# Two inverses made by VectorE between the last convolutions; triangle products of both directions together; VectorE ahead of ScalarE on the PSUM tiles of G and E

## The chip, the cores and the metric

The kernel runs on one core of a Trainium2 chip. A core has five engines with a queue each, which go on in order and wait for one another by semaphores: TensorE (PE in the profile; PEld are its weight loads), VectorE (DVE), ScalarE (ACT), GpSimd (POOL) and SyncE (SP, which here only starts DMAs). SBUF is the memory on the core, PSUM the one that TensorE writes its products into. The metric is the device time of one execution in microseconds. Before the change it is 1668.08 us, the median of three runs (1666.92 to 1673.68).

## The reference

One step of a two-branch mixer layer. 128 context tokens and 2048 latent tokens (a grid 64 wide), 1024 channels. Half of the channels go through a delta-rule recurrence in both directions (8 heads of 64), the other half through a gated short convolution; both are gated, joined and projected out.

```python
h = _rmsnorm(x, lp['norm_g']) * (1.0 + scale) + shift
proj = h @ lp['w_in']
r, k, v, g_a, b_gate, c_gate, u_conv, g_b = jnp.split(proj, IN_SPLITS, axis=-1)
...
def step(S, inp):
    r_t, w_t, k_t, v_t, kk_t, a_t = inp
    s_kk = jnp.einsum('bdhij,bdhj->bdhi', S, kk_t)
    S = (S * w_t[..., None, :] - s_kk[..., :, None] * (kk_t * a_t)[..., None, :]
         + v_t[..., :, None] * k_t[..., None, :])
    return S, jnp.einsum('bdhij,bdhj->bdhi', S, r_t)
s_final, ys = lax.scan(step, s0.astype(f32), xs)
...
yb = b_gate * _short_conv(c_gate * u_conv, lp['conv_w'], is_latent) * jax.nn.silu(g_b)
u = jnp.concatenate([ya, yb], axis=-1) @ lp['w_out']
return x + gate * u, s_final
```

The result is the normalised layer output for context and latent tokens, and the final context states S.

## The kernel before

The recurrence is computed in chunks of 64 tokens: 34 chunks for each pair of heads and each direction. Within a chunk the delta rule needs the inverse of a unit lower-triangular 64x64 matrix, made from two 32x32 inverses and a few products.

**Phase 1** projects. The tokens are cut into six blocks j (five of 384 tokens and one of 256), handled in three thirds of two blocks; in each third the four groups g of 128 channels are run through `mixA` (r, k, v and everything that the recurrence reads), `gateA`, `convB` and `gateB`. Names of PSUM tiles say what is projected: mmr, mmk, mmv, mmc, mmu, mmgb, mmb and so on; these five-slot tiles are taken in turn, so a product of one block can't start before the tile five earlier has been read. `mixA` calls `triangle` (L368) once for each direction: the products al x be of each chunk and head half, into a PSUM tile psA, each in two 64x64 quadrants of the array (`place`, L37), then three ScalarE copies into a staging tile and two DMAs to the scratch tensors scr_at (the two triangular 32x32 blocks) and scr_lo (the 32x32 block below them). In the last two thirds the list `late` is not empty; spare weight buffers then hold the staging tiles. In the last third, the convolutions and their gates of groups 1 to 3 are left for the end; beside them `early` (L1204) runs, a generator that is advanced by one step after each convolution or gate of a block.

**Phase 2** runs the recurrence in 17 stages, each with 8 chunks of both directions (gi = 0 and 1). A stage first needs its 32x32 inverses: `partI` (L886) loads the triangles of the stage (L919) and `solve` (L921) inverts them on GpSimd by elimination, two rows at a time: a product (L936) and two subtracts (L939) for each of 15 steps. The inverse goes to scr_zt (L940) and comes back as zc (L1003). Stages 0 and 1 are solved in `ahead1` during the last third, stages 2 to 4 in `early`, the rest in `main`. From the inverse and the staged operands, `partU` and `partW` make the tiles zb, F and G, `partB` X and E, and `partS` goes over the eight chunks with the state sv:

- psF -> F, one VectorE instruction (L1017); psG -> fg, four times a stage and half: for each of two tiles and two heads a ScalarE copy of one column half and a VectorE product with a mask of the other (the two lines after L1022);
- psX -> fg, four ScalarE copies with a sign; psE -> E, a ScalarE copy and a VectorE product with a mask for each tile (L1085, L1086);
- psS -> sv, the state's update on VectorE (L1123).

fg has for each direction and operand three slots, of which slot 0 holds constants, and 1 and 2 are filled in turn by even and odd stages. In `main` the order of TensorE is fixed by a string of letters (ROUND), and five PSUM slots go round for F, G, X, E, U and W; in `early`, two. Two engines that read one PSUM tile are kept in the order of the code: the second waits for the first. All the rest of the order on each engine is found by a scheduler that plans with estimated durations, so that a change in the code also moves instructions at other places.

**Phase 3** is the output projection.

Of the kernel before, what the change touches and what calls it, by code (L numbers as in the profile page):

```python
# [54 lines left out]
def phase1(K):  # L55
# [312 lines left out]
    def triangle(g, j, d, al, be, t_):  # L368

        t0, n = BLK[j]  # L370
        nch, c0 = n // 64, t0 // 64
        x, y = (be, al) if d == 0 else (al, be)
        ps = pax.tile([128, 6, 64], F32, tag="ax", name=f"psA{g}_{j}_{d}")
        for u in range(nch):
            for h in range(2):
                r = slice(h * 64, h * 64 + 64)
                T.matmul(ps[place(d, h), u, :], x[r, u * 64:u * 64 + 64], y[r, u * 64:u * 64 + 64], start=True, stop=True)  # L377
        o = t_[:, :].rearrange("p (k u i) -> p k u i", k=2, i=32)
        P.copy(o[:, :, :nch], ps[:, :nch].rearrange("p u (k i) -> p k u i", k=2))
        for r in (slice(32, 64), slice(96, 128)):  # L380
            K.mark = P.copy(o[r, 0, :nch], ps[r, :nch, 32:64]).ins
        nc.sync.dma_start(S["at"][d, g, c0:c0 + nch].rearrange("u s b j i -> (s b j) u i"), o[:, 0, :nch])
        nc.sync.dma_start(S["lo"][d, g * 128:g * 128 + 128, c0:c0 + nch], o[:, 1, :nch])

    def mixA(g, j, ws, hh, lw, pre):
# [23 lines left out]
        kds = []  # L409
        for d in range(2):  # L410
# [43 lines left out]
            triangle(g, j, d, al, be, staging(ta))  # L454
# [294 lines left out]
def phase2(K):  # L749
# [136 lines left out]
    def partI(s, after=None):  # L886

        if s < 4:
# [32 lines left out]
    def solve(s, ab, zt, tmp, dg, after):  # L921

        zf = zt[:].rearrange("p a b -> p (a b)")
        behind(G.memset(zt[:], 0.0), after)
        for h in range(2):
            G.memset(zf[h * 64:(h + 1) * 64, h:512:34], 1.0)

        G.tensor_copy(dg[:], ab[:].rearrange("p j i -> p (j i)")[:, 1:1024:66])
        G.tensor_scalar(zf[0:64, 1:512:34], dg[0:64], -1.0, None, ALU.mult)
        tv = tmp[:].rearrange("p (j m) -> p j m", m=16)  # L930
        G.tensor_tensor(tv, ab[:, :, 0:32:2], dg[:].unsqueeze(1).broadcast_to((128, 32, 16)), ALU.mult)
        G.tensor_tensor(ab[:, :, 1:32:2], ab[:, :, 1:32:2], tv, ALU.subtract)
        for m in range(15):
            j, kn, n = 2 * m, m + 1, 30 - 2 * m
            tv = tmp[:, :kn * 2 * n].rearrange("p (q r i) -> p q r i", r=2, i=n)
            G.tensor_tensor(tv, ab[:, j:j + 2, j + 2:32].unsqueeze(1).broadcast_to((128, kn, 2, n)),  # L936
                            zt[:, :kn, j:j + 2].unsqueeze(3).broadcast_to((128, kn, 2, n)), ALU.mult)
# [266 lines left out]
    def early():  # L1204
# [10 lines left out]
        for gen in (W, W, uu, uu, uu):  # L1215
            next(gen, None)
            yield
# [263 lines left out]
```

## Time and profile before

The profiled execution took 1662.38 us, of which the span from first to last instruction is 1660.6 us. The stages of it (PE idle is the window less PE's busy time):

| stretch, us | what runs | PE busy | PE clock granted |
|---|---|---|---|
| 0 to 98 | loads, modulation, norm of the first blocks | 76.4 | |
| 98 to 748 | first and middle third of phase 1 | 642.5 | |
| 748 to 921 | last third; stages 0 and 1 solved on GpSimd | 166.0 | 0.99 |
| 921 to 1000 | last convolutions and gates, with `early` | 79.0 | 1.00 |
| 1000 to 1335 | phase 2 up to its last rounds | 296.5 | 0.96 to 0.98 |
| 1335 to 1475 | last rounds, output weights prepared | 109.9 | 0.86 |
| 1475 to 1661 | output projection | 178.1 | 0.99 |
| span 1660.6, execution 1662.38 | | 1548.4 | 0.978 |

How to read the rows that follow: a row of the timeline has start, duration, engine, line, operation, out<-in, partitions x elements out<-in, the count of instructions, and in brackets the idle time before it and who ended it. Rows of one tile have min/median/max in ns and the first and last start.

### The profile page before, as it was taken

The numbers are of one execution on the slowest core, as the hardware profiler recorded it, in microseconds if no ns is written. First come the engines' busy times: TensorE is split into PE (matmuls) and PEld (weight loads), VectorE is DVE, ScalarE is ACT, GpSimd is POOL, SyncE is SP. The second block draws the span as 40 slices with busy tenths as digits, with TensorE's granted clock in tenths as the row PEclk, the third lists the DMA queues.
The fourth block names the chain that finished last, engine by engine and source line by source line (L and its number), as shares of the span: only waits on it lengthen the run. The fifth ranks groups of instructions, "written<-read, shape, count | busy, mean of one in ns | idle before, by whom it ended". The sixth has DMA issues, their size and how long they took to land.

```text
span 1660.6 us, 42386 instructions
## 1 busy us (share of the span) xinstructions
PE 1548.4 (93%) x17160; PEld 1417.8 (85%) x17160; DVE 1077.8 (65%) x2122; ACT 767.6 (46%) x1623; POOL 615.9 (37%) x1134
## 2 busy tenths in 40 slices
PE   6899999999999999999999998988889988789998
PEld 2899998999999999999988997777777877668886
DVE  5876978784638776657788534676767765574343
ACT  4544565553425454435554024666576655432222
POOL 0011221110102111112775588888888840022221
PEclk9899999999999999999999999999999979889999
DMA  9677767665746465555858859566676643264342
GB/s 378 211 258 244 254 236 265 215 227 194 217 145 207 165 207 189 188 201 179 269 177 245 273 180 272 150 184 191 171 211 157 193 135 103 65 198 149 137 146 95
DMA packets 237859, 327.23 MB, mean 197 GB/s; under 512 B 91288, under 2 KB 191896, under 8 KB 223584
## 3 DMA queue, kind: packets, MB, share of 16 engines
q1 hardware_dynamic: 231552, 318.02, 59.6%
q0 software_dynamic: 1360, 4.46, 0.7%
q8 instruction: 135, 2.21, 0.5%
q10 hardware_dynamic: 4752, 2.04, 0.5%
q14 instruction: 60, 0.49, 0.1%
HBM read 207.92 MB, written 116.54 MB: 195 GB/s over the span
## 4 chain that ended last, share of the span: by engine, by line
PE 69%; DVE 14%; ACT 7%; issue 5%; DMA 3%; POOL 0%; SPq 0%; DVEq 0%; ACTq 0%; POOLq 0%
PE psu L1351 4%; PE psu L1350 4%; PE psu L1352 4%; PE psE L834 3%; PE psS L834 3%; ACT fg L823 3%; PE psA L377 2%; PE mmc L166 2%; PE mmc L167 2%; PE mmu L166 2%; PE mmc L168 2%; PE mmu L168 2%; PE mmu L167 2%; PE psX L834 2%; PE mmv L166 2%
## 5 line engine op out<-in xcount | busy, mean ns | idle before, releaser
L939 POOL TENSOR_TENSOR zt<-zt,ztmp 128x30 f32<-128x30 f32 (+7 forms) x450 | 179.5, 399 | 35.1
L834 PE MATMUL psE<-fg 128*64 128x128 f32 x2176 | 137.4, 280 | 20.9 <-DVE fg L1025 17.2
L834 PEld LDWEIGHTS psE<-fg 128*64 128x64 f32 x2176 | 123.1, 141 | 27.3 <-issue 22.0
L834 PE MATMUL psS<-sv,E 128*64 128x64 f32 x2176 | 107.1, 236 | 25.1 <-DVE sv L1123 21.7
L834 PEld LDWEIGHTS psS<-sv,E 128*64 128x64 f32 x2176 | 83.5, 143 | 48.2 <-DVE sv L1123 38.5
L329 POOL TENSOR_TENSOR shk<-rawl 128x384 f32<-128x384 f32 (+1 forms) x24 | 24.9, 1037 | 233.8 <-ACT rawl L325 214.6
L936 POOL TENSOR_TENSOR ztmp<-ab,zt 128x60 f32<-128x60 f32 (+7 forms) x195 | 99.7, 511 | 15.3
L823 ACT ACTIVATE fg<-psX 64x512 f32<-64x512 f32 x136 | 80.5, 592 | 40.5 <-PE psX L834 38.4
L1417 POOL TENSOR_TENSOR z<-z,x 128x512 f32<-128x512 f32 x32 | 41.7, 1303 | 139.4 <-DVE z L1413 114.6
L1123 DVE TENSOR_TENSOR sv<-psS,pc 64x128 f32<-64x128 f32 x254 | 67.8, 279 | 38.8 <-PE psS L834 36.2
L1025 DVE TENSOR_TENSOR fg<-psG,consts 64x256 f32<-64x256 f32 x136 | 56.8, 418 | 47.9 <-ACT fg L825 45.1
L329 POOL TENSOR_TENSOR shv<-rawl 128x384 f32<-128x384 f32 (+1 forms) x24 | 20.4, 852 | 161.9 <-ACT rawl L325 153.7
L825 ACT COPY E<-psE 128x256 f32<-128x256 f32 x136 | 47.7, 374 | 52.6 <-PE psE L834 43.5
L166 PE MATMUL mmg<-h,w 128*128 128x384 f32 (+1 forms) x192 | 63.6, 331 | 3.7 <-ACT q1v L327 3.7
L1017 DVE TENSOR_TENSOR F<-psF,consts 128x512 f32<-128x512 f32 x68 | 44.0, 680 | 34.6 <-PE psF L834 34.6
L166 PE MATMUL mmc<-h,w 128*128 128x384 f32 (+1 forms) x192 | 64.3, 335 | 2.3 <-ACT t L423 1.8
L1086 DVE TENSOR_TENSOR E<-psE,consts 128x256 f32<-128x256 f32 x136 | 54.5, 416 | 18.2 <-ACT E L825 16.7
L825 ACT COPY fg<-psG 64x256 f32<-64x256 f32 x136 | 49.9, 367 | 33.5 <-PE psG L834 16.9
L166 PE MATMUL mmb<-h,w 128*128 128x384 f32 (+1 forms) x192 | 63.1, 329 | 1.5 <-ACT ta L436 1.5
L443 POOL COPY pcs<-pp 128x6 f32<-128x6 f32 (+1 forms) x48 | 21.5, 450 | 115.3 <-ACT pp L432 115.0
L166 PE MATMUL mmgb<-h,w 128*128 128x384 f32 (+1 forms) x192 | 63.7, 332 | 0.3 <-ACT q1r L327 0.3
L166 PE MATMUL mmv<-h,w 128*128 128x384 f32 (+1 forms) x192 | 63.4, 330 | 0.2 <-ACT q1r L327 0.2
(316 smaller groups left out, 5144.9 us busy)
## 6 DMA issues: line engine op xcount, KB each, us to landing
w<-scr_wsp SPq DMA_DIRECT2D x68, 1024.0 KB, 5.5
scr_wsp<-w SPq DMA_DIRECT2D x34, 1024.0 KB, 4.9
scr_ops<-pair SPq DMA_DIRECT2D x80, 384.0 KB, 3.0
wr<-in_win SPq DMA_DIRECT2D x34, 512.0 KB, 5.9
o<-scr_ops SPq DMA_DIRECT2D x32, 512.0 KB, 7.0
fg<-scr_ops SPq DMA_DIRECT2D x120, 128.0 KB, 5.0
x<-in_x SPq DMA_DIRECT2D x17, 512.0 KB, 3.8
wadas<-in_wada SPq DMA_DIRECT2D x8, 1024.0 KB, 13.5
```

Source lines behind the costliest of these rows:

```text
L166: T.matmul(ps[:, :n], w[:, 0, k], hh[:, 0, k, :n], start=k == 0, stop=False)
L167: T.matmul(ps[:, :n], w[:, 0, k], hh[:, 1, k, :n], start=False, stop=False)
L168: K.dense = T.matmul(ps[:, :n], w[:, 1, k], hh[:, 0, k, :n], start=False, stop=k == 7).ins
L823: P.activation(dst, src, AF.Copy, scale=-1.0)
L825: P.copy(dst, src)
L834: r = T.matmul(*a, start=True, stop=True, **k)
L936: G.tensor_tensor(tv, ab[:, j:j + 2, j + 2:32].unsqueeze(1).broadcast_to((128, kn, 2, n)), zt[:, :kn, j:j + 2].unsqueeze(3).broadcast_to(( ...
L939: O.solved = G.tensor_tensor(zt[:, :kn, j + 2:32], zt[:, :kn, j + 2:32], tv[:, :, r], ALU.subtract).ins
L1123: r = V.tensor_tensor(dst, sp[gi][0:64, q], B.pc[0:64, d, 2 * p:2 * p + 2, c:c + 1].broadcast_to((64, 2, 64)), ALU.mult)
L1350: T.matmul(ps[:], mh[:, n], hi[:, cs], start=start and n == 0, stop=False)
L1351: T.matmul(ps[:], mh[:, n], lo[:, cs], start=False, stop=False)
L1352: T.matmul(ps[:], ml[:, n], hi[:, cs], start=False, stop=stop and n == 3)
```

## The change

Three edits.

- `triangle` becomes `triangles`: it takes a list of directions and makes their products by turns, chunk by chunk and head by head. In the first third it is still called once for each direction; from the middle third on, once for both.
- `solve` becomes a generator for an engine to be named. GpSimd's solves use it as before. `by_vector` runs it on VectorE for stages 3 and 4 in `early`, with slot 2 of fg as scratch memory; the store of the inverse goes to SP's queue. GpSimd solves 2 and then 5 there, and 6 on in `main`.
- In the evacuation of psG and of psE the VectorE product stands ahead of the ScalarE copy.

```diff
-    def triangle(g, j, d, al, be, t_):
+    def triangles(g, j, todo):
...
         for u in range(nch):
+            us = slice(u * 64, u * 64 + 64)
             for h in range(2):
                 r = slice(h * 64, h * 64 + 64)
-                T.matmul(ps[place(d, h), u, :], x[r, u * 64:u * 64 + 64], y[r, u * 64:u * 64 + 64], start=True, stop=True)
+                for p_, (d, al, be, _) in zip(ps, todo):
+                    x, y = (be, al) if d == 0 else (al, be)
+                    T.matmul(p_[place(d, h), u, :], x[r, us], y[r, us], start=True, stop=True)
...
-            triangle(g, j, d, al, be, staging(ta))
+            todo.append((d, al, be, staging(ta)))
+            if not late or d:
+                triangles(g, j, todo)
+                todo = []
...
-    def solve(s, ab, zt, tmp, dg, after):
+    def solve_steps(eng, s, ab, zt, tmp, dg, after):
...
         for m in range(15):
             j, kn, n = 2 * m, m + 1, 30 - 2 * m
             tv = tmp[:, :kn * 2 * n].rearrange("p (q r i) -> p q r i", r=2, i=n)
-            G.tensor_tensor(tv, ab[:, j:j + 2, j + 2:32].unsqueeze(1).broadcast_to((128, kn, 2, n)),
-                            zt[:, :kn, j:j + 2].unsqueeze(3).broadcast_to((128, kn, 2, n)), ALU.mult)
+            eng.tensor_tensor(tv, ab[:, j:j + 2, j + 2:32].unsqueeze(1).broadcast_to((128, kn, 2, n)),
+                              zt[:, :kn, j:j + 2].unsqueeze(3).broadcast_to((128, kn, 2, n)), ALU.mult)
             for r in range(2):
-                O.solved = G.tensor_tensor(zt[:, :kn, j + 2:32], zt[:, :kn, j + 2:32], tv[:, :, r], ALU.subtract).ins
-        G.dma_start(S["zt"][s].rearrange("h u s b q i -> (h u s b) (q i)"), zf)
+                last = eng.tensor_tensor(zt[:, :kn, j + 2:32], zt[:, :kn, j + 2:32], tv[:, :, r], ALU.subtract).ins
+            if m % 4 == 0:
+                yield
+        if eng is G:
+            O.solved = last
+        (G.dma_start if eng is G else D)(S["zt"][s].rearrange("h u s b q i -> (h u s b) (q i)"), zf)
+
+    def by_vector(s, d):
+
+        x = [B.fg[d][:, k, 2].rearrange("p h u t -> p (h u t)") for k in range(2)]
+        ab = x[0].rearrange("p (j i) -> p j i", i=32)
+        load_I(s, ab, K.dense)
+        yield
+        yield from solve_steps(V, s, ab, x[1][:, 0:512].rearrange("p (a b) -> p a b", b=32), x[1][:, 512:1024],
+                               O.rI.tile([128, 16], F32, tag="dgv", name=f"dgv{s}", bufs=1), K.dense)
...
+                    V.tensor_tensor(g.gs[H[1 - h], g.op, h, us], ps[gi][r, :, 64:128], B.mG[r, g.d].unsqueeze(1).broadcast_to((64, 4, 64)), ALU.mult)
                     copy(g.gs[H[1 - h], 0, h, us], ps[gi][r, :, 0:64])
-                    V.tensor_tensor(g.gs[H[1 - h], g.op, h, us], ps[gi][r, :, 64:128], B.mG[r, g.d].unsqueeze(1).broadcast_to((64, 4, 64)), ALU.mult)
...
+                    V.tensor_tensor(to(H[1]), of(H[1]), B.mE[:, g.d].unsqueeze(1).broadcast_to((128, 4, 64)), ALU.mult)
                     copy(to(H[0]), of(H[0]))
-                    V.tensor_tensor(to(H[1]), of(H[1]), B.mE[:, g.d].unsqueeze(1).broadcast_to((128, 4, 64)), ALU.mult)
...
         partI(2)
         B.back = O.solved
+        vec = (x for k in range(2) for x in by_vector(3 + k, k))
+        next(vec)
         yield
         sts[0] = partL(0, K.dense)
-        yield
-        partI(3, K.dense)
+        next(vec)
         yield
         W, uu, bb = partW(0, sts[0]), partU(0, sts[0]), partB(0, sts[0])
         for gen in (W, W, uu, uu, uu):
             next(gen, None)
+            next(vec, None)
+            next(vec, None)
             yield
-        partI(4, B.back)
+        partI(5, B.back)
         for gen in (bb, W, W):
             next(gen, None)
+            next(vec, None)
             yield
+        for _ in vec:
+            pass
```

How this moves instructions, at three places.

VectorE, among the last convolutions, around the masked copies of G of stage 0 (pv, ob, vcarry belong to the convolutions; F and psG to stage 0). Before:

```order
L541 COPY pv_4_10219<-vcarry 128x128
L1017 TENSOR_TENSOR F_10158<-psF_0_0_10140,consts 128x512
L1017 TENSOR_TENSOR F_10160<-psF_1_0_10141,consts 128x512
L535 TENSOR_TENSOR pv_4_10219<-ct_4_10191,mmu_10193 128x384
L88 TENSOR_SCALAR ob_4_10218<-pv_4_10219,dv 128x384
L550 COPY vcarry<-pv_4_10219 128x128
L517 SCALAR_TENSOR_TENSOR ob_4_10218<-pv_4_10219,dv,ob_4_10218 128x384
L519 SCALAR_TENSOR_TENSOR ob_4_10218<-pv_4_10219,dv,ob_4_10218 128x384
L1025 TENSOR_TENSOR fg_9816<-psG_0_0_10226,consts 64x256
```

In the changed kernel (fg_9816 and fg_9817 on both sides of the arrow are the scratch of stage 3's and stage 4's inverse):

```order
L950 TENSOR_TENSOR fg_9816<-fg_9816 128x8x16
L547 COPY pv_4_10247<-vcarry 128x128
L942 TENSOR_TENSOR fg_9817<-fg_9817,dgv_10256 128x512
L947 TENSOR_TENSOR fg_9816<-fg_9816 128x252
L943 TENSOR_TENSOR fg_9817<-fg_9817 128x512
L950 TENSOR_TENSOR fg_9816<-fg_9816 128x9x14 x2
L947 TENSOR_TENSOR fg_9816<-fg_9816 128x240
L1048 TENSOR_TENSOR fg_9816<-psG_0_0_10141,consts 64x256
L1048 TENSOR_TENSOR fg_9817<-psG_1_0_10142,consts 64x256
L950 TENSOR_TENSOR fg_9816<-fg_9816 128x10x12
L1048 TENSOR_TENSOR fg_9816<-psG_0_0_10141,consts 64x256
```

The first inverse is spread between the evacuations, F stands behind its first half, and psG's evacuation stands ahead of the next convolution's mmu where it stood behind it. On TensorE the products of psF and psG moved with this: psF now stands within a gate's products mmb and psG within the next convolution's mmc, where each stood behind a whole projection.

SP, from the second of the last convolutions on (w are weights, scr_zt the inverses, ob the convolutions' results). Before:

```order
L127 DMA w_891_10508<-scr_wsp 128x2048
L919 DMA ab_10572<-scr_at 32x1024 x3
L127 DMA w_892_10510<-scr_wsp 128x2048
L883 DMA a_9813<-scr_lo 128x256 x2
L581 DMA scr_mixT<-ob_4_10218 128x384
L127 DMA w_903_10742<-scr_wsp 128x2048
L127 DMA w_904_10744<-scr_wsp 128x2048
```

In the changed kernel:

```order
L955 DMA scr_zt<-fg_9816 128x512
L925 DMA o_9815<-scr_at 32x1024
L127 DMA w_891_10646<-scr_wsp 128x2048
L882 DMA o_9814<-scr_ops_57 128x2x512
L127 DMA w_892_10648<-scr_wsp 128x2048
...
L955 DMA scr_zt<-fg_9817 128x512
L127 DMA w_899_10823<-scr_wsp 128x2048
L998 DMA fg_9817<-scr_ops_58 64x2x256 x2
L127 DMA w_900_10825<-scr_wsp 128x2048
```

The two stores, which wait for VectorE's last instruction of an inverse, now stand ahead of two pairs of weight loads. The loads of fg from scr_ops, which fill slot 2 for stage 1, stood earlier in the queue; they now come behind the stores, since slot 2 is the scratch.

VectorE, in the middle of phase 2 (one round: E and sv of one stage, F and G of the next). Before:

```order
L1025 TENSOR_TENSOR fg_9816<-psG_0_0_13529,consts 64x256
L1123 TENSOR_TENSOR sv_13004<-psS_0_0_13555,pc 64x128
L1025 TENSOR_TENSOR fg_9817<-psG_1_0_13530,consts 64x256
L1123 TENSOR_TENSOR sv_13006<-psS_1_0_13561,pc 64x128
L1031 STREAM_TRANSPOSE zr_13567<-zc_13504 128x512
L1025 TENSOR_TENSOR fg_9816<-psG_0_0_13529,consts 64x256
L1025 TENSOR_TENSOR fg_9817<-psG_1_0_13530,consts 64x256
```

In the changed kernel:

```order
L1048 TENSOR_TENSOR fg_9816<-psG_0_0_13584,consts 64x256
L1048 TENSOR_TENSOR fg_9817<-psG_1_0_13585,consts 64x256
L1147 TENSOR_TENSOR sv_13059<-psS_0_0_13610,pc 64x128
L1147 TENSOR_TENSOR sv_13061<-psS_1_0_13616,pc 64x128
L1048 TENSOR_TENSOR fg_9816<-psG_0_0_13584,consts 64x256
L1055 STREAM_TRANSPOSE zr_13622<-zc_13559 128x512
L1048 TENSOR_TENSOR fg_9817<-psG_1_0_13585,consts 64x256
```

Both first parts of G stand together ahead of the two sv; the first of them now waits for TensorE where it waited for ScalarE.

More of the change, by code (lines that the diff above doesn't have):

```diff
@@ L408, in mixA @@
         rS = shifted(psr or dense(wr_, hh, n, "r"), j, 0, g, "r", 1)
-        kds = []
+        kds, todo = [], []
         for d in range(2):
@@ L886, in partI @@
     def partI(s, after=None):
-        if s < 4:
+        if s < 6:
             ab = B.hold[s % 2][:].rearrange("p k u t -> p (k u t)").rearrange("p (j i) -> p j i", i=32)
@@ L1232, in main @@
         sts[2] = partL(2, K.first)
-        partI(5, K.first)
+        partI(6, K.first)
         next(bb)
         sts[LA] = partL(LA, K.first)
-        partI(6, O.solved)
+        partI(7, O.solved)
         tail = iter(())
@@ L1272, in main @@
                 sts[s + LA + 1] = partL(s + LA + 1)
-            if 1 <= s and s + 6 < NST:
-                partI(s + 6)
+            if 1 <= s and s + 7 < NST:
+                partI(s + 7)
         for f in pend:
```

31 lines of the change are left out of this document (17 added, 14 removed).

## The prediction

> **What bounds the kernel now.** I read the page first: TensorE (PE) is busy 93% of the span, but its share of the chain that ended last is smaller, so some stage is bound by something else.
>
> ```profile
> PE 1548.4 (93%) x17160; PEld 1417.8 (85%) x17160; DVE 1077.8 (65%) x2122; ACT 767.6 (46%) x1623; POOL 615.9 (37%) x1134
> PE 69%; DVE 14%; ACT 7%; issue 5%; DMA 3%; POOL 0%; SPq 0%; DVEq 0%; ACTq 0%; POOLq 0%
> ```
>
> Then the busy time by stage (window; its length; PE, PEld, DVE, ACT, POOL; clock).
>
> ```profile
> 748.00:921.00 173.00, 166.03 (x1363) 161.82 (x1362) 134.74 (x232) 83.33 (x203) 94.81 (x158) 0.99 0.71 225
> 921.00:1000.00 79.00, 79.00 (x768) 76.66 (x768) 31.33 (x68) 11.99 (x26) 58.82 (x126) 1.00 0.66 213
> 1000.00:1024.00 24.00, 18.92 (x471) 16.60 (x473) 10.56 (x31) 11.14 (x24) 20.67 (x48) 0.98 0.99 288
> 1100.00:1335.00 235.00, 209.83 (x5364) 185.21 (x5362) 161.68 (x402) 149.84 (x316) 202.88 (x447) 0.98 0.68 185
> 1335.00:1475.00 140.00, 109.87 (x2094) 94.63 (x2091) 83.09 (x188) 69.57 (x139) 24.00 (x39) 0.86 0.39 115
> ```
>
> Phase 1 is PE's own pace; between 921 and 1000 us, the last convolutions, PE has no idle time at all, so anything that holds it there is lost. In phase 2 PE is idle about a tenth of the time, and more at the end, where its clock falls too. The waits of 1000 to 1480 us (total, times, longest) say on whom:
>
> ```profile
> PE psS L834 <- DVE sv L1123: 21.7, 35, 2.1
> PE psE L834 <- DVE fg L1025: 17.2, 9, 3.6
> DVE fg L1025 <- ACT fg L825: 45.1, 30, 3.2
> DVE E L1086 <- ACT E L825: 16.7, 23, 3.0
> ```
>
> PE waits for VectorE, and VectorE had itself waited for ScalarE's half of the same PSUM tile.
>
> **The triangle products.** The last third has both directions side by side already, the middle third has them apart.
>
> ```profile
> 748.12 0.33 PE L166 MATMUL mmv<-h,w 128*128 128x384 f32 x1
> 748.29 0.34 PE L167 MATMUL mmv<-h,w 128*128 128x384 f32 x1
> 748.56 1.44 PE L377 MATMUL psA<-pair,pair 64*64 64x64 f32 x48
> 749.93 0.45 PE L210 MATMUL psb<-hshb,onr 128*128 128x384 f32 x1
> 750.21 0.34 PE L211 MATMUL psb<-hslb,onr 128*128 128x384 f32 x1
> ...
> 1239.51 1.05 PE L834 MATMUL psF<-fg,o 64*64 64x128 f32 x32
> 1241.99 0.69 PE L834 MATMUL psS<-sv,E 128*64 128x64 f32 x16
> ```
>
> Dense products start 0.17 us apart; going to the 64x64 products takes 0.27 and coming back 0.28, so a round trip costs 0.2 us. Joining the directions saves one for each of the middle third's 8 blocks: **1.6 us**. Interleaving them uses four quadrants of the array instead of two. psA goes at 1.44/48 = 30 ns a record; psF, in four quadrants already, at 33 ns; psS, which alternates column halves, at 43. So I see no gain from more quadrants: 0. Bounds: 704 of the 1088 records lie in these two thirds (22 of 34 chunks); at half of 30 ns that is -10, and if pairs of products with the same rows go at psS's pace, 704 x 13 ns = +9. I take **-1.5**. The joined products also wait for the second direction's operand: the first direction's are issued later, and their two copies on ScalarE and two stores with them; these feed only the inverses, of which the first begin after 800 us, so this costs nothing in the middle third, and in the last third the two directions stand together in both versions.
>
> **The two inverses on VectorE.** Those of stages 3 and 4 leave POOL for VectorE, between the last convolutions. One inverse has 15 products, 30 subtracts and two steps of 512 elements, 47 instructions with two SBUF inputs and 6064 elements a partition, and five small ones. Their price by the nearest rows, and GpSimd (POOL) beside them:
>
> ```profile
> 899.04 0.42 DVE L407 TENSOR_TENSOR sq<-kk,sq 128x256 f32<-128x256 f32 x1
> 661.55 0.55 DVE L441 TENSOR_TENSOR pair<-or,pp 128x384 f32<-128x384 f32 x1
> 874.50 0.97 DVE L441 TENSOR_TENSOR pair<-or,pp 128x384 f32<-128x384 f32 x1
> ...
> 874.15 0.90 POOL L936 TENSOR_TENSOR inv<-inv 128x252 f32<-128x252 f32 x1
> L939 POOL TENSOR_TENSOR zt<-zt,ztmp 128x30 f32<-128x30 f32 (+7 forms) x450 | 179.5, 399 | 35.1
> L936 POOL TENSOR_TENSOR ztmp<-ab,zt 128x60 f32<-128x60 f32 (+7 forms) x195 | 99.7, 511 | 15.3
> ```
>
> 0.42 and 0.55 give 0.15 us and 1.0 ns an element: 7.1 + 6.2, with 0.03 us each for an instruction that needs the one before and 1.3 for the small ones, 16 us an inverse, 32 for two, in a window where VectorE has 79 - 31 = 48 us free. Alone they would fit. But the third row is the second one's instruction while a POOL solve runs: 0.42 us longer, until about the end of the POOL instruction that began at 874.15. VectorE now solves beside POOL, whose instructions take 0.4 to 0.5 us. An instruction that comes late in a POOL instruction waits little, so I take 0.13 us each (bounds 0 and 0.42): 94 x 0.13 = 12, so 32 + 12 = 44 us.
>
> The Trainium skill, "SBUF — State Buffer", section "Who interferes with whom", has the rule that speaks against this edit: a VectorE instruction with two SBUF inputs is shut out while GpSimd reads SBUF, for the whole instruction. The row of 0.97 us agrees. By the rule in full, at 0.42 each, the two inverses take 32 + 39 = 71 us and the second ends some 27 us later than by my sum.
>
> What stands behind them:
>
> ```profile
> 935.10 1.10 PE L834 MATMUL psF<-fg,o 64*64 64x128 f32 x32
> 936.27 1.27 DVE L1017 TENSOR_TENSOR F<-psF,consts 128x512 f32<-128x512 f32 x2
> 988.99 0.33 PE L166 MATMUL mmb<-h,w 128*128 128x384 f32 x1
> ...
> w<-scr_wsp SPq DMA_DIRECT2D x68, 1024.0 KB, 5.5
> ```
>
> First, in VectorE's queue, both F evacuations and the gate's evacuations stand behind some 25 solve instructions. F ended at 937.5; now the first inverse starts near 930, and 25 x 0.46 plus the evacuations between put it near 944. psG needs those PSUM slots and its products now stand inside the next convolution, near 939: PE waits about 5 us. Second, in SyncE's (SP) queue the second inverse's store waits for the solve, and behind it stand the next convolution's weights w_899 and w_900, with a load between that also waits for the store to land. Start 930, 44 us of solves, 12 of older work between: the second ends near 986; the store lands near 990.5 (such stores take 4.2 us, the row below), w_900 is issued near 992 and lands 5.5 us later, at 997.5. Its products, mmb, started at 988.99: PE is 8 us late, and the first stall is contained in it. In 1000 to 1024 us the DMA engines are at 0.99 and PE idles 5 us for them; I give back 1.5. **+6.5**; bounds: +2 with no contention (the solves end near 974, F alone is late), +33 with 0.42 each.
>
> POOL loses two solves. Does that pay?
>
> ```profile
> L940 POOL DMA_DIRECT2D scr_zt<-zt x15: 608/617/617, 957.3 to 1349.2; - x15
> DMA to landing us min/median/max: 2.4/4.2/9.1
> ...
> L1003 SPq DMA_DIRECT2D zc<-scr_zt x32: 597/611/3402, 968.5 to 1403.2; - x32
> ...
> L1003 SPq DMA_DIRECT2D zc<-scr_zt x4: 611/644/3402, 968.5 to 1029.2; - x4
> ```
>
> The last inverse is stored at 1349 and read at 1403; the first of the fifteen, stage 2's, is stored at 957 and read by the last of the four loads up to 1029. POOL was not waited for, so its two solves fewer bring 0. The inverse of stage 5, the next that POOL makes, can't begin before SP has issued its loads, one of which now stands behind the first VectorE store; that leaves POOL idle for some us near 960, which thins the contention a little, and its result is needed three stages later than stage 2's.
>
> **VectorE ahead of ScalarE.** A round of phase 2:
>
> ```profile
> 1240.97 1.09 PE L834 MATMUL psG<-fg,o 64*64 64x128 f32 x28 [0.19 <-ACT fg L823]
> 1242.04 1.32 ACT L1048 ACTIVATE zb<-zc,consts 128x512 f32<-128x512 f32 x2
> 1243.39 1.23 ACT L825 COPY fg<-psG 64x256 f32<-64x256 f32 x3
> 1243.79 0.43 DVE L1025 TENSOR_TENSOR fg<-psG,consts 64x256 f32<-64x256 f32 x1 [1.89 <-ACT fg L825]
> 1244.25 0.28 DVE L1123 TENSOR_TENSOR sv<-psS,pc 64x128 f32<-64x128 f32 x1
> 1245.01 0.28 DVE L1123 TENSOR_TENSOR sv<-psS,pc 64x128 f32<-64x128 f32 x1
> 1245.84 0.84 DVE L1025 TENSOR_TENSOR fg<-psG,consts 64x256 f32<-64x256 f32 x2
> L1178 DVE TENSOR_TENSOR y<-y,yss x17: 671/691/2715, 1080.8 to 1477.7; 128x512 f32<-128x512 f32 x17
> ```
>
> psG is done at 1242.06, but ScalarE is in zb until 1243.36, so VectorE starts at 1243.79. In the new order VectorE takes both first parts by 1242.95 and both sv by 1243.55; the chain ends with a ScalarE copy near 1245.4 instead of VectorE's at 1246.68. So psS gets its sv some 1.2 us earlier and the slot is free 1.2 earlier. In such a round PE waited 0.16 and 0.31 for sv: about 0.5 saved in 13 rounds, 6 us. Of the 9 psE stalls (17.2 us) I take 1 us each, 9. Against it: where VectorE is the later engine, ScalarE's copies now wait for it, and behind them on ScalarE the next copies and zb; and y, 0.69 us, moves ahead of an F evacuation in about three rounds and holds up F, then sv, by up to 1.4: together -5. **-10**; bounds -20 (most of the 17.2 goes, and the clock of the last window comes back) and +4.
>
> **Sum:** -1.5 + 6.5 - 10 = -5. The profiled execution took 1662.38 us (span 1660.6 and 1.8 around it), so 1657.4 by its own time; it lies 5.7 below the runs' median of 1668.08. A difference carries over: **1663**.
>
> **Rivals.** *The POOL wait decides, slower.* At 0.27 us each (between the quiet row and the 0.97 one) the solves take 57 us, the second ends near 999, w_900 lands near 1010.5, and PE is 21 late, 20 after the cover: -1.5 + 20 - 10 = +8.5, 1676.5. The decision lies where the solves cost 11.5, at about 0.18 each. For it: the row of 0.97; against: only an instruction that starts early in a POOL one pays that much, and POOL's steps are short. At 0.42 each it would be -1.5 + 33 - 10 = +21.5, 1689.5; I give that end 0.04 of this rival's chance. It is what the rule of the Trainium skill's "SBUF — State Buffer" gives if each instruction meets a whole one of POOL's. *The stalls go wholly.* Solves +4, triangles -1.5, reorder -19: 1651.5. For it: 45.1 us of VectorE's waits are for ScalarE alone; against: PE then waits for sv, which needs its own psS. *The reorder does nothing*, since the tile needs both engines anyway and only the order of the two changes: -1.5 + 6.5 = +5, 1673.
>
> **How the numbers follow.** A measurement of this kernel tells about 0.5%, 8.3 us, from no change. Forecast 0.38 (of it 0.13 faster, 0.25 same; its own range 1656 to 1669); stalls wholly gone 0.26 (faster); POOL wait 0.20 (0.15 slower, 0.05 same); reorder nothing 0.16 (0.11 same, 0.05 slower). Faster 0.39, same 0.41, slower 0.20. The range, 1648 to 1681, reaches into both outer cases and leaves out the far ends of the bounds.
>
> **What would show it.** Solves: VectorE rows of the inverse between 930 and 990, 0.2 to 0.5 us each, longer than 0.15 + 1.0 ns an element; a PE stall at psG near 939 and one for a weight load near 990. Reorder: the wait of VectorE's fg for ScalarE gone, and psE's for fg well under 17.2. Triangles: psA still near 30 ns a record, with fewer switches in the middle third. I am wrong if the second inverse ends before 975 or after 1000, or if PE's idle time between 1000 and 1475 us doesn't fall.

## The result, and the profile after

The changed kernel takes 1656.07 us, the median of 5 runs (1655.21 to 1658.96), against 1666.92 for the kernel before in the same comparison: ratio 0.9947, 95% interval 0.9924 to 0.9971, by the ratio 8.8 us less (4.8 to 12.7). The profiled execution took 1657.8 us (span 1656.0), 1.7 over that median; the kernel before was profiled in one of 1662.38 us, 4.5 under its own. So the two profiles lie 4.6 us apart where the runs lie 8.8 apart.

The page after, busy time by engine and the shares of the chain that ended last:

```profile
PE 1538.7 (93%) x17160; PEld 1412.4 (85%) x17160; DVE 1108.4 (67%) x2226; ACT 766.8 (46%) x1623; POOL 569.0 (34%) x1028
...
PE 47%; DVE 10%; ACT 7%; DMA 4%; issue 3%; POOL 3%; SPq 0%; DVEq 0%; ACTq 0%; POOLq 0%
```

TensorE is 9.7 us less busy, VectorE has 31 us more and GpSimd 47 less. The stretches after (window; its length; PE, PEld, DVE, ACT, POOL; clock):

```profile
748.00:921.00 173.00, 165.80 (x1331) 161.99 (x1330) 135.00 (x230) 81.11 (x201) 92.13 (x156) 0.98 0.73 229
921.00:1000.00 79.00, 73.75 (x707) 71.06 (x706) 64.84 (x168) 11.55 (x25) 52.67 (x106) 0.96 0.66 208
1000.00:1024.00 24.00, 21.15 (x462) 19.21 (x460) 10.85 (x32) 10.40 (x23) 7.56 (x17) 1.00 0.92 249
1100.00:1335.00 235.00, 209.79 (x5518) 188.00 (x5510) 165.94 (x411) 153.53 (x321) 187.40 (x415) 0.98 0.70 187
1335.00:1475.00 140.00, 113.01 (x2068) 95.50 (x2067) 82.20 (x192) 69.50 (x139) 11.93 (x15) 0.87 0.40 117
```

Among the last convolutions, 921 to 1000 us, TensorE was busy without a gap; now it idles 5.25 us and its granted clock fell from 1.00 to 0.96. From 1000 to 1475 us it idles 63.0 us where it idled 68.6. The same events, compared by when they come in the two traces, place the change: the copies of psA come 0.8 us later than before at 373 us; the first copy of an mmc of the last convolutions comes 4.3 earlier, at 906.6 instead of 911.0; the last convolution's product comes 4.4 later near 1000; the first zr of the scan (VectorE's transpose of an inverse) 2.4 later near 1013; a result of the output projection, VectorE's last z from psu, 5.5 earlier near 1488. So in this pair of traces the triangles brought about 5 us, the inverses took 6.7 away (4.3 + 2.4), and the reorder brought 7.9.

**Triangles.** TensorE's timeline at the start of the last third, after:

```profile
745.62 0.34 PE L167 MATMUL mmv<-h,w 128*128 128x384 f32 x1
745.89 0.94 PE L379 MATMUL psA<-pair,pair 64*64 64x64 f32 x48
746.76 0.44 PE L210 MATMUL psb<-hshb,onr 128*128 128x384 f32 x1
```

48 products, now over four quadrants, go in 0.87 us from start to next start, 18 ns a record (one matmul instruction). Before, the same row was 1.44 us, 1.37 to the next start, 28.5 ns. In the middle third, two runs of 24 records at 0.84 us each became one of 48 at 0.87. Added up over both thirds, the products with the switch behind them take 13.7 us where they took 22.8. The waits from 98 to 748 us (in all, times, longest), after:

```profile
PE mmc L166 <- ACT q1r L327: 4.1, 4, 1.2
```

That wait was 0.5 us in one case before: the copies of both directions now stand together ahead of q1r, a scaled copy of the projected r, on ScalarE.

**Inverses.** TensorE in the scan's first stage, after (start, duration; in brackets the idle time ahead and who ended it):

```profile
940.18 2.77 PE L840 MATMUL psG<-fg,o 64*64 64x128 f32 x32 [3.92 <-DVE F L1041]
942.88 0.69 PE L167 MATMUL mmc<-h,w 128*128 128x384 f32 x1
943.36 0.52 PE L168 MATMUL mmc<-h,w 128*128 128x384 f32 x1
943.68 0.52 PE L166 MATMUL mmc<-h,w 128*128 128x384 f32 x1
...
945.51 0.34 PE L166 MATMUL mmc<-h,w 128*128 128x384 f32 x1
945.68 0.34 PE L167 MATMUL mmc<-h,w 128*128 128x384 f32 x1
```

and VectorE's evacuation of F:

```profile
939.45 0.68 DVE L1041 TENSOR_TENSOR F<-psF,consts 128x512 f32<-128x512 f32 x1
...
940.24 0.68 DVE L1041 TENSOR_TENSOR F<-psF,consts 128x512 f32<-128x512 f32 x1
```

psG waits 3.9 us for F, which stands behind the first half of an inverse in VectorE's queue. Then its 32 products take 2.77 us where they took 1.10 elsewhere, and the dense products behind it start 0.32 us apart, not 0.17, until 945.3: some 2.8 us more. With psF's own 1.3 us that makes 8. Some 2 came back between 1000 and 1013 us; from 1000 to 1024 the DMA engines are at 0.92.

**Reorder.** The waits of 1000 to 1480 us, after:

```profile
ACT E L831 <- DVE E L1109: 27.9, 47, 2.5
...
ACT fg L831 <- DVE fg L1048: 22.9, 29, 1.6
PE psS L840 <- DVE sv L1147: 18.4, 30, 1.7
...
PE psE L840 <- ACT fg L831: 15.2, 9, 3.3
...
DVE fg L1048 <- ACT fg L831: 11.7, 18, 1.6
...
PE psT L847 <- DVE y L1202: 4.4, 1, 4.4
```

VectorE's 45.1 us for ScalarE's half of G fell to 11.7; ScalarE now waits 22.9 for VectorE there and 27.9 at E. PE's wait for sv fell from 21.7 to 18.4 us and the one of psT, a transpose of the results, for y from 9.1 to 4.4. psE's wait hardly fell (17.2 to 15.2), but changed its engine.

### The profile page after: what moved, and what is told of

Read it like the earlier page. It is cut to its first block, busy times and chain, and to the rows that moved or that the text cites. A ratio compares the mean times of both kernels' runs of the same rounds, so it can differ in the third digit from the quotient of the medians.

```text
span 1656.0 us, 42386 instructions
## 1 busy us (share of the span) xinstructions
PE 1538.7 (93%) x17160; PEld 1412.4 (85%) x17160; DVE 1108.4 (67%) x2226; ACT 766.8 (46%) x1623; POOL 569.0 (34%) x1028
## 4 chain that ended last, share of the span: by engine, by line
PE 47%; DVE 10%; ACT 7%; DMA 4%; issue 3%; POOL 3%; SPq 0%; DVEq 0%; ACTq 0%; POOLq 0%
PE psu L1380 4%; PE psu L1381 4%; PE psu L1382 4%; PE psE L840 3%; PE psS L840 2%; ACT fg L829 2%; PE psX L840 2%; PE psW L840 1%; PE mmg L166 1%; PE mmg L168 1%; PE mmg L167 1%; PE mmc L166 1%; PE mmc L167 1%; PE mmu L167 1%; PE mmu L166 1%
## 5 line engine op out<-in xcount | busy, mean ns | idle before, releaser
L950 POOL TENSOR_TENSOR zt<-zt,ztmp 128x30 f32<-128x30 f32 (+7 forms) x390 | 153.3, 393 | 30.6
L840 PE MATMUL psE<-fg 128*64 128x128 f32 x2176 | 135.8, 278 | 17.4 <-ACT fg L831 15.2
L840 PE MATMUL psS<-sv,E 128*64 128x64 f32 x2176 | 99.5, 235 | 19.3 <-DVE sv L1147 18.4
L1147 DVE TENSOR_TENSOR sv<-psS,pc 64x128 f32<-64x128 f32 x254 | 63.9, 277 | 43.6 <-PE psS L840 41.4
L947 POOL TENSOR_TENSOR ztmp<-ab,zt 128x60 f32<-128x60 f32 (+4 forms) x165 | 85.1, 516 | 12.9
L1048 DVE TENSOR_TENSOR fg<-psG,consts 64x256 f32<-64x256 f32 x136 | 57.3, 421 | 24.0 <-ACT fg L831 11.7
L166 PE MATMUL mmg<-h,w 128*128 128x384 f32 (+1 forms) x192 | 64.3, 335 | 3.8 <-ACT q1v L327 3.8
L831 ACT COPY E<-psE 128x256 f32<-128x256 f32 x136 | 48.4, 373 | 37.8 <-DVE E L1109 27.9
L168 PE MATMUL mmg<-h,w 128*128 128x384 f32 (+1 forms) x192 | 64.0, 334 | 0.0
```

The lines of the kernel that those rows point to most:

```text
L166: T.matmul(ps[:, :n], w[:, 0, k], hh[:, 0, k, :n], start=k == 0, stop=False)
L168: K.dense = T.matmul(ps[:, :n], w[:, 1, k], hh[:, 0, k, :n], start=False, stop=k == 7).ins
L831: P.copy(dst, src)
L840: r = T.matmul(*a, start=True, stop=True, **k)
L947: eng.tensor_tensor(tv, ab[:, j:j + 2, j + 2:32].unsqueeze(1).broadcast_to((128, kn, 2, n)), zt[:, :kn, j:j + 2].unsqueeze(3).broadcast_to ...
L950: last = eng.tensor_tensor(zt[:, :kn, j + 2:32], zt[:, :kn, j + 2:32], tv[:, :, r], ALU.subtract).ins
```

## The experiments

Ratios are medians of a kernel's runs to those of the kernel before on the same chip, with the 95% interval; 1% is 16.7 us. The first question was whether each edit acts at its own place and the terms add up (theory 1), or whether the gain lies in phase 2 alone, in GpSimd's freed time or in one edit (theory 2).

### One edit at a time, and two

Triangles alone: `triangle` becomes `triangles` as in the change, the rest as before.

> The triangle products of both directions together, nothing else changed. Theory 1 (each edit acts at its own place and the three add up): 48 psA records in 0.87 us instead of 1.37 or twice 0.84, so about 5 us less in all (0.997 of before), with a new wait of mmc for ScalarE's q1r of about 4 us in the middle third that eats part of some 10 us. Theory 2 (the gain of the change lies in phase 2 alone): within 2 us of before.

Measured: 1657.79 us, ratio 0.9935 (0.9914 to 0.9955), -10.8 us.

Inverses alone: `solve_steps`, `by_vector` and the calls of `early` and `main` as in the change, the rest as before.

> The two inverses on VectorE, nothing else changed. Theory 1: PE waits about 5 us at psF and psG of stage 0 and runs some 3 us at half clock behind it, and 2 us of that come back at 1000 us: 6 to 7 us slower (1.004 of before). Theory 2 (the later stages gain because POOL makes two inverses fewer): phase 2 is shorter by some 5 us even with the old order of VectorE and ScalarE, so the whole is within 2 us of before.

Measured: 1672.99 us, ratio 1.0033 (1.0009 to 1.0056), +5.5 us.

Reorder alone: the two exchanged pairs of lines.

> VectorE ahead of ScalarE on psG and psE, nothing else changed. Theory 1: phase 2 shorter by about 8 us (0.995 of before), psE's wait now for ScalarE's last copy and hardly shorter, psS's and psT's waits shorter. Theory 2: the wait only changes its engine, 2 us or less.

Measured: 1655.41 us, ratio 0.9931 (0.9907 to 0.9954), -11.5 us.

Triangles and reorder, with all inverses on GpSimd:

> The change without the two inverses on VectorE. Theory 1: the sum of the two gains, about 13 us below before (0.992), and 6 to 7 below the changed kernel. Theory 2: no faster than the changed kernel, since the inverses on VectorE are part of what gains in phase 2.

Measured: 1651.44 us, ratio 0.9899 (0.9866 to 0.9932); again, beside other kernels on another chip:

> The same kernel as the one without inverses on VectorE (triangles and reorder), again, beside the two above on one chip. Theory 1: ratio 0.990 as the first time (0.9866 to 0.9932), at or below the whole change with F first. Theory 2: the whole change with F first lies clearly above it, by 0.3% or more.

Measured: 1649.42 us, ratio 0.9882 (0.9852 to 0.9912).

What follows: two edits make the kernel faster and one slower, each by more than its interval. That the terms add up is not shown: alone they add to -1.01%, the whole change measured -0.53%, which lies at the edge of the intervals; triangles and reorder add to -1.34% and measured -1.01% together. A gain in phase 2 alone is ruled out by the triangles. Leaving the inverses where they were gives -1.0 to -1.2%: a version ahead of both kernels. The inverses on VectorE cost 0.3% alone and 0.5 to 0.65% by the difference between the change and this version. That single profiles can't carry such sums shows here: the profile of the reorder alone was taken in an execution of 1662.24 us, 6.8 above that kernel's median, the one before in one 4 to 6 below.

All the traces together part the edits better than one pair does. The first mmc copy of the last convolutions starts at 906.6 to 911.9 us in the five with joined triangles and at 910.2 to 913.8 in the nine without, 3.5 us apart in the mean. From there to the first zr, the five with two inverses on VectorE and GpSimd solving beside them take 106.4 to 109.3 us, the seven without 101.3 to 106.0. From the first zr to the last y (VectorE's product with yss), the six with the new order at G take 452.8 to 462.8 us, six with the old one 464.2 to 468.5 (two more runs with the old order, with a single inverse and with GpSimd kept away, take 472.4 and 482.1). So the inverses and the reorder part the traces each in its own stretch, the triangles only in the mean, and a single trace can lie several us off.

### Which half of the reorder

```diff
 psG alone:
+                    V.tensor_tensor(g.gs[H[1 - h], g.op, h, us], ...)
                     copy(g.gs[H[1 - h], 0, h, us], ps[gi][r, :, 0:64])
-                    V.tensor_tensor(g.gs[H[1 - h], g.op, h, us], ...)
 psE alone:
+                    V.tensor_tensor(to(H[1]), of(H[1]), ...)
                     copy(to(H[0]), of(H[0]))
-                    V.tensor_tensor(to(H[1]), of(H[1]), ...)
```

> Of the reorder alone only the half on G's tiles: VectorE's copy of a tile of psG is written ahead of ScalarE's, the tiles of E stay as before. Theory 1 (the gain sits where VectorE stood longest for ScalarE, and that was fg for fg, 45.1 us in 30 waits before): this half holds most of the reorder's 11 us, ratio about 0.995, and the trace has VectorE's wait of fg for ScalarE's fg near 12 us while E for E stays near 17. Theory 2 (the 9 waits of psE are the price, and who comes first there decides it): this half alone leaves PE's waits of psE for VectorE's fg near 17 us, ratio 0.998 to 1.000.

Measured: 1659.51 us, ratio 0.9937 (0.9910 to 0.9963).

> The other half alone: VectorE's copy of a tile of E's is written ahead of ScalarE's, the tiles of G stay as before. Theory 1: E for E was only 16.7 us in 23 waits, so at most 2 to 3 us are to be had, ratio 0.998 to 1.000, and VectorE's wait of fg for ScalarE's fg stays near 45 us. Theory 2: this half holds the gain, ratio about 0.995, with PE's waits for sv and E below the 21.7 us of before. If both ratios lie near 0.995 and the two together give 0.993, either half takes the same wait away.

Measured: 1666.22 us, ratio 0.9975 (0.9955 to 0.9994). The waits of 1000 to 1480 us, of G alone (two rows), then of E alone (four):

```profile
PE psS L834 <- DVE sv L1123: 16.0, 15, 2.3
...
DVE fg L1024 <- ACT fg L825: 9.6, 15, 1.6
```

```profile
ACT E L825 <- DVE E L1085: 65.0, 67, 3.2
DVE fg L1025 <- ACT fg L825: 46.3, 30, 3.2
...
PE psS L834 <- DVE sv L1123: 30.3, 70, 2.2
...
PE psE L834 <- DVE fg L1025: 17.2, 9, 3.7
```

G's half holds most of the gain, and with it alone VectorE's wait at G falls to 9.6 us and PE's for sv from 21.7 to 16.0. E's half leaves both that wait and psE's as they were, and in its profile PE waits longer for sv, not less; its small gain is at the edge of what was measured. So the edit's place was VectorE's wait at G, not the stall of psE.

### What the inverses on VectorE cost

GpSimd kept from solving beside VectorE: its solves of stages 2 and 5 stand behind VectorE's second store.

```diff
-        partI(2)
-        B.back = O.solved
...
-        partI(5, B.back)
...
         for _ in vec:
             pass
+        partI(2, O.stored)
+        partI(5, O.solved)
```

> The two inverses on VectorE alone, with POOL's two solves beside them moved behind VectorE's second inverse, so that POOL does not compute while VectorE solves. Theory 1 (the price is VectorE's lateness at the evacuation of F, made of the 25 solve instructions ahead of it and 0.17 us more for each beside POOL, and then a lower clock): the solve instructions shrink to within 0.02 us of 0.15 us + 1.0 ns an element, F comes about 4 us earlier, PE's wait at psG for F falls from 1.4 us (3.9 in the changed kernel) to under 0.5 us, and the time is within 2 us of before, ratio 0.999 to 1.002, against 1.0033 with POOL beside it. Theory 2 (the price is the amount of work that VectorE takes over, or the store and loads behind it, contention or not): ratio still about 1.003. A third way is that POOL's two solves, now about 40 us later, hold a stage of the last scan up: then PE waits for lw or a weight load behind 1000 us that before does not have, and the ratio is over 1.003.

Measured: 1691.39 us, ratio 1.0125 (1.0093 to 1.0157). VectorE's groups of solve instructions from 920 to 980 us (busy, mean ns), with the two inverses alone:

```profile
L944 DVE TENSOR_TENSOR fg<-fg 128x110 f32<-128x110 f32 (+7 forms) x53 | 18.9, 364 | 0.9
L941 DVE TENSOR_TENSOR fg<-fg 128x192 f32<-128x192 f32 (+7 forms) x27 | 14.4, 534 | 0.5
```

and with GpSimd kept away:

```profile
L944 DVE TENSOR_TENSOR fg<-fg 128x30 f32<-128x30 f32 (+7 forms) x60 | 14.6, 250 | 1.1
L941 DVE TENSOR_TENSOR fg<-fg 128x60 f32<-128x60 f32 (+7 forms) x30 | 10.3, 344 | 0.5
```

The first evacuation of F in the timeline of the one and of the other:

```profile
946.49 0.68 DVE L1035 TENSOR_TENSOR F<-psF,consts 128x512 f32<-128x512 f32 x1
```

```profile
941.86 1.28 DVE L1035 TENSOR_TENSOR F<-psF,consts 128x512 f32<-128x512 f32 x2
```

GpSimd's company costs a subtract 0.11 us and a product 0.19 on average, 0.14 over both ((60 x 0.114 + 30 x 0.19)/90). Without it F comes 4.6 us earlier and psG doesn't wait for it. The worst case is a short instruction that meets a long one, in the changed kernel's timeline VectorE's first product beside GpSimd's 512-element step:

```profile
927.69 1.46 DVE L947 TENSOR_TENSOR fg<-fg 128x60 f32<-128x60 f32 x1
...
927.76 1.31 POOL L942 TENSOR_TENSOR ztmp<-o,dgp 128x512 f32<-128x512 f32 x1
```

With GpSimd kept away the same product takes 0.20 us. The Trainium skill, "SBUF — State Buffer", section "Who interferes with whom", says that such an instruction is shut out for the whole of GpSimd's; the row agrees in length, since VectorE ends 0.08 us behind GpSimd's instruction, though its record begins 0.07 us ahead of it. The mean of 0.14 us lies far below that worst case.

The time as a whole went much like the third way of the expectation, at another place than it named. GpSimd's first solve here runs from 985 to 1012 us (from 925 in the changed kernel). SP, which has a load into that solve's buffer o next, issues nothing from 1003.5 to 1012.0, and ScalarE's queue stands from its first load of pc at 1004.75 to its second at 1016.2, with the evacuation of E behind it:

```profile
1004.75 11.98 ACTq L807 DMA_DIRECT2D pc<-scr_pc  x2
...
1021.59 1.20 ACT L825 COPY E<-psE 128x256 f32<-128x256 f32 x4 [16.89 <-DMA sv<-scr_vt]
```

(In the program's order the load of o and the second load of pc wait by the same DMA semaphore, which would tie the one to the other; no run tested it.) PE waits 11.3 us there, so this run tells what GpSimd's company does to VectorE, and nothing of the total.

Only stage 3 on VectorE:

```diff
-        vec = (x for k in range(2) for x in by_vector(3 + k, k))
+        vec = by_vector(3, 0)
...
-        partI(5, B.back)
+        partI(4, B.back)
```

> Only the first of the two inverses (stage 3) on VectorE, the second back on POOL and all later stages on POOL as before. Theory 1 (lateness at F): F stands behind the first inverse's instructions, not the second's, so nearly the whole price stays, ratio 1.002 to 1.003, with a wait at psG for F as in the two-inverse kernel. Theory 2 (amount of work): half the price, ratio about 1.0015, and no wait at psG.

Measured: 1676.95 us, ratio 1.0042 (1.0015 to 1.0068). One inverse costs no less than two. But this is not half of the change: the scheduler put F behind all but the last five of the fifteen steps of the one inverse (F at 956.26 us), psG waited 5.2 us for F and the convolution 3.5 for VectorE. The run speaks against a price that goes with the amount of work and agrees with one that goes with F's lateness, here a greater one than in the change.

F first, in the whole change and with the inverses alone:

```diff
+            if eng is V and m == 2:
+                behind(r_, O.early)
```

Here r_ is the third step's product and O.early F's second evacuation in stage 0.

> The whole change, with one more order on VectorE: from the third step of each inverse on (128x156 and later), the solve instructions stand behind the two evacuations of F of the first scan stage, so 6 instead of 23 solve instructions of steps 1 to 15 stand ahead of F (psF was done at 932.5 us and F came at 939.45 in the changed kernel). Theory 1 (the price of the inverses on VectorE is F's lateness and the lower clock behind it): F comes 3 to 5 us earlier, PE's wait at psG for F falls from 3.9 us to under 1.5 us, the matmuls behind it keep their spacing of 0.17 us, and 4 to 7 us come back: ratio to before about 0.990 to 0.992, level with the kernel that has no inverses on VectorE. Theory 2 (the price is in the amount of work on VectorE, or in stages and queues behind it): ratio stays at 0.994 to 0.996 although F is early, with the loss found behind 1000 us.

Measured: 1652.67 us, ratio 0.9900 (0.9868 to 0.9931). F comes at 936.16 instead of 939.45 us, psG no longer waits, and its products take 1.12 us instead of 2.77. But psF now waits 1.9 us for its loads where it waited 1.3, and the half pace comes behind it instead, from 935.4 to 938.3 us. From the first mmc copy to the first zr the lateness is 3.9 us (from -1.7 to +2.2 against the trace before) instead of 6.7.

> The two inverses on VectorE alone, with the same extra order (F ahead of the third step). Theory 1: most of the 5.5 us that the inverses cost alone is gone, ratio 0.999 to 1.001. Theory 2: still about 1.003. If POOL's 47 us of freed time were worth anything to the rest, the ratio would come out under 0.998.

Measured: 1672.53 us, ratio 1.0027 (1.0005 to 1.0048). Here theory 1's number missed: the wait at psG is gone, but psF now waits 3.9 us and runs at half pace, and the first zr is still 5.2 us late. The reason that I then saw is on ScalarE's queue. The operand loads of stage 0 are issued just when VectorE ends the inverse's 128x512 subtraction; timeline rows of VectorE and ScalarE in the changed kernel, then of both and TensorE in this one:

```profile
926.99 0.67 DVE L943 TENSOR_TENSOR fg<-fg 128x512 f32<-128x512 f32 x1
...
927.73 2.56 ACTq L998 DMA_DIRECT2D fg<-scr_ops  x4
```

```profile
932.52 0.68 DVE L937 TENSOR_TENSOR fg<-fg 128x512 f32<-128x512 f32 x1
...
933.27 2.60 ACTq L994 DMA_DIRECT2D fg<-scr_ops  x4
...
938.73 2.26 PE L834 MATMUL psF<-fg,o 64*64 64x128 f32 x32 [3.88 <-DVE sgb L564]
```

In all six kernels with inverses on VectorE that I had by then, loads follow that end within 0.1 us (in the one with a single inverse, two of the stage's loads go out before). One load fills slot 1 for both operands, and the solve's data lies in slot 2 of the first, between them in memory: an access that spans it. The last run splits each load in two, so that none spans it:

```diff
-                D(dst, src[:, p * 128 + h * 64:...].rearrange("k c t -> c k t"))
+                for k in range(2):
+                    D(dst[:, k], src[k, p * 128 + h * 64:...])
```

> The two inverses on VectorE alone with F first, and the operand loads of the first scan stage on ScalarE's queue split into one per buffer half, so that no load spans the strip of fg in which VectorE solves. Theory 1, with its second place (psF comes late because those loads, in front of two evacuations on ScalarE's queue, are issued only within 0.1 us of the end of the first inverse's 128x512 subtraction, as in all six kernels with inverses on VectorE): the loads go out near 922 us instead of 933, psF waits under 1 us instead of 3.9 and runs its 32 records in 1.1 us instead of 2.3, and the first zr behind 1000 us comes within 2 us of where it stands before the change (5.2 us late without the split); ratio 0.998 to 1.001. Theory 2 (the amount of work on VectorE, or the queues behind 950 us): the loads are early and psF does not wait, but zr at 1013 is still 4 to 6 us late and the ratio stays near 1.003.

Measured: 1673.79 us, ratio 1.0039 (1.0014 to 1.0063). Half of the expectation held: the loads go out from 922.96 us on, and no longer behind the solve. The number missed again. TensorE's rows in it:

```profile
928.60 1.09 PE L834 MATMUL psF<-fg,o 64*64 64x128 f32 x18
...
934.02 1.94 PE L834 MATMUL psF<-fg,o 64*64 64x128 f32 x14 [3.31 <-DMA fg<-scr_ops]
```

The scheduler moved psF up by 10 us, trusting the earlier loads, and these took 6.5 us (median) to land while the DMA engines were at 0.93; so psF stopped for 3.3 us in its middle. The first zr is 5.1 us late, as theory 2 said. The wait on the solve is shown as the cause of the late loads; that its removal pays is not.

## Why the prediction came out as it did

**The total: inside the range, partly by luck.** -5 us was forecast and -8.8 (4.8 to 12.7 less) measured. The triangles were worth more than their term, by 2 to 9 us as told below, and the parts measured alone add to -16.8, about twice what the whole gave. So the sum came near without its terms being right. Of the signs that the prediction named, the end of the second inverse (976.7 us, inside 975 to 1000), the stall at psG, most of the end of VectorE's wait at G (45.1 to 11.7) and PE's shorter idle time from 1000 to 1475 us (63.0 instead of 68.6) came; the stall for a weight load, psE's far shorter wait and psA near 30 ns a record did not.

**Triangles: the direction right, the size wrong.** The step that failed is "I see no gain from more quadrants: 0". Its price came from other tiles in four quadrants, psF at 33 ns; but those have 128 columns, and psA's 64 go at 18 ns when the quadrants alternate, against 28.5 to 35 before. By the rows, records and switches together give 9.1 us; the wait for q1r takes 3.6 back, which leaves 5.5, and the pair of traces shows 5. The direct measurement gives -10.8 (-14.3 to -7.5) for a predicted -1.5, at the end of the bounds that I had named. The step from the reorder alone (0.9931) to triangles and reorder (0.9899), on the same chip, is only 5.3 us, near the rows but with wide intervals. So the traces bear out 3.5 to 5.5 us; where the rest up to 10.8 lies, or whether it is there, no trace shows.

**Inverses: the sum right, its second half wrong.** F's lateness came as worked out: a stall at psG near 939 us, put at 5, was 3.9 at 940.18. The price of GpSimd's company, put at 0.13 us an instruction, measured 0.14, and the two inverses ended at 976.7 us, 9 before the 986 that I took, in part since they began 5 us earlier; they are out of the queue in time, and no stall for a weight load near 990 exists. "The first stall is contained in it" therefore did not happen: the stall at F was the price. What took the place of the 8 us for w_900 was TensorE's slower pace behind the stall, 2.8 us, and psF's own wait. That the sum agrees is luck in this half: +6.5 was forecast; +6.7 stands in the traces, +5.5 (1.5 to 9.3) was measured alone, and 8 to 11 by the difference from the version without them. The rival in which GpSimd's company decides, at 0.27 us each, is refuted by the 0.14. (The prediction's 6064 elements an inverse are 6464 by its own steps, 0.4 us more, which decides nothing.) That GpSimd's two solves fewer bring nothing holds: no kernel with inverses on VectorE is ahead of the one without.

**Is F the cause?** With F first in the whole change, 0.9947 became 0.9900, level with the version without the inverses (0.9882 on the same chip, 0.9899 on another); the intervals overlap, so its size is not tight. The traces place only some 3 us of it where the edit acts, between the first mmc copy and the first zr. From there to the last y the trace with F first is 5.8 us shorter than that of the change, although VectorE, ScalarE and GpSimd go through the same instructions in the same order up to about 1400 us; that part is not explained by F. In the kernel with the inverses alone the same edit changed nothing that can be measured (1.0033 to 1.0027): psF's wait grew from 2.8 to 3.9 us, and with its loads split psF stopped again, for 3.3. The ratios of these two runs are those of theory 2, the amount of work or the queues behind. Shown is that TensorE's stalls in stage 0 move with VectorE's and ScalarE's queues there. Whether the price is in these stalls stays open.

**Reorder: the size right, the terms not.** -10 was forecast, -7.9 stands in the pair of traces, -11.5 (-15.5 to -7.7) was measured alone. But of the 17.2 us of psE I took 9 as gain, and 2 to 3 came: 15.2 in the change, 13.9 with the reorder alone. PE's wait for sv fell by 3.3 us in the change and 7.0 with the reorder alone, psT's for y by 4.7 in both; no single wait holds the gain. VectorE's wait at G is the place where the edit acts, since G's half alone gives 0.9937 of the whole 0.9931. Both rivals on the reorder are out: the stalls of psE did not go, and the reorder alone is clearly faster.

## What to carry to other kernels

Free time on an engine is not a price of nothing: ask what stands behind the moved work in that queue, and whose storage it borrows, since here 48 us of free VectorE time hid the work and not the 4 us by which it held TensorE. Where two engines read one PSUM tile in turn, try first the one whose queue is waited for next. And when a change has several parts, time each alone: one of them may be giving back what the others bring.

## What the runs showed of the hardware

A short stall cost TensorE little beyond itself, a longer one half its pace for a while. Duration of a record (min/median/max ns) of psF and psG behind their stalls, first in the changed kernel (psF had waited 1.3 us, psG 3.9), then with F first in it (psF 1.9), then with the inverses and F first alone (psF 3.9):

```profile
L840 PE MATMUL psF<-fg,o x32: 269/269/320, 930.8 to 932.2; 64*64 64x128 f32 x32
...
L840 PE MATMUL psG<-fg,o x32: 417/417/473, 940.2 to 942.5; 64*64 64x128 f32 x32
```

```profile
L840 PE MATMUL psF<-fg,o x32: 269/269/418, 934.1 to 935.4; 64*64 64x128 f32 x32
```

```profile
L834 PE MATMUL psF<-fg,o x32: 414/417/472, 938.7 to 940.6; 64*64 64x128 f32 x32
```

Stalls of 1.3 and 1.4 us left 269 ns and the usual pace behind (the 32 records themselves took 1.64 and 1.89 us, where 1.10 is usual); those of 2.8 and 2.9 us (inverses alone, and with GpSimd kept away) and of 3.9 left a median of 417. The stall of 1.9 us (F first) lies between: psF's median stays at 269, but from its last records on the pace is halved, and the dense products behind it start 0.21 us apart, not 0.12, until 938.3 us, at a granted clock of 0.50:

```profile
935.77 0.58 PE L167 MATMUL mmb<-h,w 128*128 128x256 f32 x1
936.14 0.41 PE L168 MATMUL mmb<-h,w 128*128 128x256 f32 x1
936.36 0.41 PE L166 MATMUL mmb<-h,w 128*128 128x256 f32 x1
```

In the run with a single inverse, too, products ran at full pace for 1.5 us behind a stall of 3.5 us, and at half from 942.4 to 945.8. So the half pace can begin later than the stall ends. The Trainium skill, "TensorE: Matmul & The Clock Gate", section "What's actually happening", has half rate after at least one idle window of about 3.4 us; here 1.9 us was enough, and the measurement decides.

64x64 products with 64 columns start 18 ns apart when four quadrants take turns (48 in 0.87 us), and 28.5 to 35 when one direction's two quadrants come behind the other's (48 in 1.37 us) or alone (24 in 0.84).
